# Odd chunks' inverse products on the other column half, six VectorE steps behind read-outs, and a shorter last unit in a FoX/RWKV-7 hybrid block

## The chip, the cores and the metric

The kernel runs on one core of a Trainium2 chip. Its engines work side by side, each through its own queue in order: TensorE (PE, with its weight loads as PEld), VectorE (DVE), ScalarE (ACT), GpSimd (POOL), and SyncE (SP), which mostly issues DMA transfers. The metric is the device time of one execution in microseconds; lower is better. The kernel before ran three times: 1635.21 (the median), 1632.43 and 1638.53 us.

## The reference

A transformer block for one sequence of 1024 tokens and width 1024: a token mixer with two branches (attention with a forget gate, and RWKV-7), gates, an output projection, and a feed-forward network with a short convolution. The change lies in the RWKV-7 branch, which has 8 heads of 64:

```python
def rwkv7_time_mix(p, mu, w0, w2, a0, a2, g2, k_k, k_a, r_k, ln_w, ln_b):
    p = p + (token_shift(p) - p) * mu
    r, k, v, xw, xa, xg = _split(p, RWKV_SPLITS)
    ...
    kk = heads(k * k_k)
    kk = kk / jnp.maximum(jnp.sqrt(jnp.sum(kk * kk, axis=-1, keepdims=True)), L2_EPS)
    k_mod = k.astype(jnp.float32) * (1 + (a - 1) * k_a)
    ...
    def step(state, inp):
        r_t, w_t, k_t, v_t, a_t, b_t = inp
        sa = jnp.einsum('bhvk,bhk->bhv', state, a_t)
        state = state * w_t[:, :, None, :] + sa[..., None] * b_t[:, :, None, :] + v_t[..., None] * k_t[:, :, None, :]
        y_t = jnp.einsum('bhvk,bhk->bhv', state, r_t)
        return state, y_t
    ...
    _, y = lax.scan(step, state0, ...)
    mean = jnp.mean(y, axis=-1, keepdims=True)
    var = jnp.mean(jnp.square(y - mean), axis=-1, keepdims=True)
    y = ((y - mean) * lax.rsqrt(var + GN_EPS)).reshape(bsz, seq, RWKV_WIDTH) * ln_w + ln_b
    bonus = (jnp.sum(r_h * k_h * r_k, axis=-1, keepdims=True) * v_h).reshape(bsz, seq, RWKV_WIDTH)
    return ((y + bonus) * g).astype(p.dtype)
```

## The kernel before

**Stages.** The span of 1632.7 us has a start with the modulation and the first projections (to about 160 us), the RWKV-7 chunk stage (about 160 to 622), attention (to about 815), and then the merge, the output projection and the feed-forward network. The change touches the chunk stage, and with the head loads at its end the start of attention.

**Units.** The recurrence isn't run step by step. The sequence is cut into chunks of 64 tokens, and within a chunk the recurrence becomes matrix products with the inverse of a unit triangular 64x64 matrix. The work goes in 8 units, numbered k = 0 to 7: four pairs p of heads, and for each the two halves hf of the sequence (8 chunks, `NCU`). The two heads of a pair lie on partitions 0 to 63 and 64 to 127 (`HS[0]`, `HS[1]`). The numbers in tile names give p and then the half or the chunk; the order's names end in a serial number.

**`pre`** (L745 to L875) prepares a unit. VectorE scales the keys and the decays (`kr`, `ar`, `al`, `bk`, and the bonus' `rkb`, which lies in the tile `ksq`). The products `p` of bk and ar give E, E's 32x32 diagonal blocks go by DMA through memory (`sm`, `M`), and 31 pairs of small VectorE steps (`t` at L828, `E` at L832) invert them in place. The inverse's blocks go back by DMA (`se`, `TT`). The transposes `vt`, `at`, `tb` and the product `q` fill UV and QA.

**`main`** (L877 to L985) finishes the inverse (`X`, `xi`, `zi`), multiplies it with QA (`uw`, L907 to L919), and copies one half of the result to Wt (VectorE) and the other to UV (ScalarE). Then come `mz` (which reads Wt), the chain of states (`sp`, `S`), the output `yp`, and the head-wise mean and variance (`mu`, `va`). `head_sums` splits a tile into a rounded part (`hi`, ScalarE; Ztr, Zts) and the rest (`lo`, L735; Wtr, Wts) and multiplies both by the block matrix `blk_r`.

**uw before.** For a chunk c and a head half h, rows `HS[h]` go to columns `HS[h]`: chunks 0 to 3 to one PSUM bank, 4 to 7 to the other. The trace lists each of these fp32 products as two records.

**What sets the order.** TensorE's order is the program's own: `Weave` interleaves the steps of `pre` and `main` with filler (the projections `ps_rkv`, `qk`, `v`, `gt`), and a generator's `yield x` lets some x ns of modelled filler pass first. The order of the other engines in this stage is set by a scheduler within the dependences; `tc.add_manual_dep(..., NOSYNC)` adds a dependence of order alone, with no wait on a semaphore between engines. `marks` holds the last instruction of a kind ("S", "E", "bank", "QA", "y") to which X is ordered. `evac_done` is called on each read-out of a filler's PSUM bank (`k`, `r`, `v` at L410, `vs` at L1002): the steps in `soft` that were emitted within the last 3000 modelled ns are ordered behind it.

The head loads `stA`, `stB` and `vh` of attention are issued from GpSimd's queue (L1043 to L1047), which also runs `lo` and the copies `hi_in` at L303.

Of the kernel before, what the change touches and what calls it, by code (L numbers as in the profile page):

```python
# [12 lines left out]
ALU = mybir.AluOpType  # L13
# [3 lines left out]
S = 1024  # L17
# [5 lines left out]
CH = 64  # L23
# [111 lines left out]
def hybrid_block(ctx: ExitStack, tc: tile.TileContext, a, out):  # L135
# [4 lines left out]
    def mm(o, lhsT, rhs, start, stop, more=False):  # L140

        weave.mm_cost(o, lhsT, rhs)
        nc.tensor.matmul(o, lhsT, rhs, start=start, stop=stop, skip_group_check=more)  # L143
# [5 lines left out]
    def f32(ap):  # L149
        return ap.bitcast(F32)  # L150
# [17 lines left out]
    def V(name, i=0, n=1):  # L168
        o, _ = VEC[name]
        return vec[:, o + i : o + i + n]  # L170
# [83 lines left out]
    def evac_done(i):  # L254
        for x, t in soft:
            if weave.now - t < 3000:
                tc.add_manual_dep(x.ins, i.ins.name, NOSYNC)
        soft.clear()
        return i
# [127 lines left out]
    with ExitStack() as es:  # L387
# [7 lines left out]
        def gen(name):  # L395
            return pr.tile([128, NH], F32, tag="gen", name=name)
# [318 lines left out]
        def c3(ap):  # L715
            return ap.rearrange("p (c s) -> p c s", s=CH)
# [13 lines left out]
        def head_sums(ps, x, hi, lo, behind_it=False):  # L730

            i = nc.scalar.copy(hi, x)
            if behind_it:
                behind_state(i)
            nc.gpsimd.tensor_tensor(lo, x, f32(hi), op=ALU.subtract)  # L735
            yield 3400
            mm(ps, blk_r, hi, start=True, stop=False)
            mm(ps, blk_r, lo, start=False, stop=True)

        def pre(k, p, hf):  # L740
# [40 lines left out]
            stt(kr, kr, V("k_k", p), al, op0=ALU.mult, op1=ALU.mult)  # L781
            tt(bk[:, :, 0, :], c3(kr), c3(en), op=ALU.mult)
            nc.gpsimd.tensor_copy(bk[64:128, :, 2, :], bk[64:128, :, 0, :])
            tt(ar[:, 1], c3(rr), el[:, :, 1:], op=ALU.mult)
            soft.clear()
            soft.append((ts(al, al, V("k_a", p), oka[:, p : p + 1], op0=ALU.mult, op1=ALU.add), weave.now))
            soft.append((tt(al, al, kk, op=ALU.mult), weave.now))
            soft.append((tt(bk[:, :, 1, :], c3(al), c3(en), op=ALU.mult), weave.now))
# [3 lines left out]
            stt(rkb, rr, V("r_k", p), al, op0=ALU.mult, op1=ALU.mult)  # L792
# [84 lines left out]
        def main(k, p, hf):  # L877
# [10 lines left out]
            for h in range(2):  # L888
                i = nc.vector.transpose(X[B0[h], :, :], TT[B0[h], :, 0:32])
                for x in ("S", "E", "bank") if k == 0 else ("S", "E", "QA") if k > 4 else ("S", "E"):  # L890
                    if x in marks:
                        tc.add_manual_dep(i.ins, marks[x].ins.name, NOSYNC)
# [17 lines left out]
            for c0 in range(0, NCU, 4):  # L910
                ps = gen(f"uw{n}{c0}")
                for c in range(c0, c0 + 4):
                    for h in range(2):
                        x = (c - c0) * 128
                        mm(ps[HS[h], x : x + 128], TT[HS[h], c, :], QA[HS[h], c, :, :], start=True, stop=True)
                pv = ps.rearrange("p (c a s) -> p c a s", a=2, s=CH)
                nc.vector.tensor_copy(Wt[:, c0 : c0 + 4, :], pv[:, :, 1, :])
                for h in range(2):
                    nc.scalar.copy(UV[HS[h], c0 : c0 + 4, h, :], pv[HS[h], :, 0, :])  # L919
# [44 lines left out]
            def part(nm, i):  # L964
                return rw.tile([128, NH], F32R, tag=nm, name=f"{nm}{i}{n}", bufs=1)
# [3 lines left out]
            yield from head_sums(mu, y, part("Zt", "r"), part("Wt", "r"))  # L969
            stt(y, mu, -1.0 / CH, y, op0=ALU.mult, op1=ALU.add)  # L970
            ysq = rw.tile([128, NH], F32, tag="ysq", name=f"ysq{n}", bufs=1)
            nc.scalar.activation(ysq, y, AF.Square)
            yield 2700
            va = gen(f"va{n}")
            yield from head_sums(va, ysq, part("Zt", "s"), part("Wt", "s"))
# [1150 lines left out]
```

## Time and profile before

| | |
|---|---|
| three runs, us | 1635.21, 1632.43, 1638.53 |
| the profiled execution, us | 1634.44 |
| its span in the trace, us | 1632.7 |
| mean granted TensorE clock | 0.996 |
| busy: TensorE, VectorE, ScalarE, GpSimd, us | 1598.9, 1211.9, 827.9, 155.5 |
| uw: products by the trace, us of one | 256 records, 0.269 |
| Wt copies: count, us of one | 16, 0.418 |

The profile is one execution. A row of the timeline gives the start, the duration of the group, engine, line, operation, out <- in, form and count; in brackets follows how long the engine was idle before it and what released it. In the form "64*64" is the part of TensorE's array that a product uses, rows by columns. A row of the groups gives the durations in ns (minimum, median, maximum). The chain of waits goes back from the last instruction to whatever released each step, so what stands in it set the time there; what doesn't had room.

### The profile page before, as it was taken

The page shows a single profiled execution, that of the slowest core. Times are in us where ns is not written, and L with a number is a line of the kernel's source. Part 1 is how long each engine was busy: PE and PEld are TensorE (multiplying, and loading weights), DVE is VectorE, ACT ScalarE, POOL GpSimd, SP SyncE. Part 2 cuts the span into 40 slices and gives each one's busy share as a digit, 9 for nine tenths or more (in the row PEclk, how much of TensorE's full clock was granted, in tenths as well). Part 3 has the DMA queues.
Part 4 walks back from the last instruction along what each step waited for, and adds up shares of the span by engine and source line. Part 5 has one row for each costly group of instructions (what it writes and reads, how often), then busy time and mean ns, then how long its engine had stood idle before and what let it go on. Part 6 is the DMA issues. An engine that isn't in the chain of part 4 may idle for free.

```text
span 1632.7 us, 25956 instructions
## 1 busy us (share of the span) xinstructions
PE 1598.9 (98%) x9678; PEld 1334.0 (82%) x9678; DVE 1211.9 (74%) x2343; ACT 827.9 (51%) x1557; POOL 155.5 (10%) x189
## 2 busy tenths in 40 slices
PE   7899999999999999999999999999999999999998
PEld 7777878888978788888888888888888888888886
DVE  4786787878876526878669548987777777886677
ACT  5563344544455656778623235644444444555455
POOL 0011111112111011333122000000000000000000
PEclk9999999999999999999999999999999999999999
DMA  9397645543333336434197511233322322675363
GB/s 341 120 337 206 178 132 148 136 117 93 112 106 95 98 126 161 130 108 123 49 345 277 189 70 39 78 129 102 118 97 97 110 98 97 237 246 162 123 213 110
DMA packets 123543, 238.79 MB, mean 146 GB/s; under 512 B 42189, under 2 KB 51285, under 8 KB 123417
## 3 DMA queue, kind: packets, MB, share of 16 engines
q1 hardware_dynamic: 114936, 218.77, 41.1%
q0 software_dynamic: 8480, 18.37, 4.2%
q8 instruction: 76, 1.25, 0.3%
q14 instruction: 51, 0.41, 0.1%
HBM read 172.57 MB, written 64.50 MB: 145 GB/s over the span
## 4 chain that ended last, share of the span: by engine, by line
PE 70%; DVE 7%; DMA 2%; ACT 2%; issue 2%; SPq 1%; POOL 0%; DVEq 0%; POOLq 0%; ACTq 0%
PE X L143 15%; PE D L143 13%; PE Y L143 7%; PE wo L143 5%; PE br L143 5%; PE gt L143 5%; PE W L143 4%; PE ps_rkv L143 3%; PE rk_ps L143 3%; PE ov L143 2%; PE lg L143 2%; PE tp L147 1%; DMA stB<-d_st 1%; DVE E L832 1%; DVE t L828 1%
## 5 line engine op out<-in xcount | busy, mean ns | idle before, releaser
L143 PE MATMUL D<-op,op 128*128 128x512 f32 x924 | 209.8, 389 | 0.0
L143 PEld LDWEIGHTS D<-op,op 128*128 128x128 f32 x924 | 173.3, 188 | 36.3 <-DVE op L1327 0.3
L143 PE MATMUL X<-T_m,S 128*128 128x512 f32 x440 | 107.1, 390 | 0.0
L143 PEld LDWEIGHTS X<-T_m,S 128*128 128x128 f32 x440 | 82.5, 188 | 17.7 <-ACT T_m L1809 0.5
L1326 ACT CAST op<-g 128x512 fp32r<-128x512 f32 x77 | 47.8, 621 | 72.9 <-PE D L143 47.6
L1327 DVE TENSOR_TENSOR op<-g,op 128x512 fp32r<-128x512 f32 x77 | 53.0, 689 | 41.2 <-ACT op L1326 41.2
L1588 DVE SCALAR_TENSOR_TENSOR c<-ab,vec,c 128x512 f32<-128x512 f32 x88 | 65.8, 750 | 18.4 <-ACT c L1591 16.8
L828 DVE TENSOR_TENSOR t<-E,M 128x60 f32<-128x60 f32 (+24 forms) x248 | 55.5, 224 | 24.3 <-DMA M<-sm 17.6
L1554 DVE TENSOR_TENSOR A<-ur,A 128x512 fp32r<-128x512 f32 x64 | 44.0, 689 | 38.3 <-ACT A L1550 38.2
L1554 DVE TENSOR_TENSOR S<-ur,S 128x512 fp32r<-128x512 f32 x66 | 45.5, 691 | 35.2 <-ACT S L1550 35.1
L1550 ACT CAST S<-ur 128x512 fp32r<-128x512 f32 x66 | 41.1, 622 | 57.3 <-DVE ur L1543 30.4
L311 DVE TENSOR_TENSOR lo_in<-raw_in,hi_in 128x512 fp32r<-128x512 f32 x84 | 57.6, 725 | 16.0 <-PE gt L143 4.8
L143 PE MATMUL Y<-T_h,A 128*128 128x512 f32 x264 | 63.4, 389 | 0.0
L143 PE MATMUL Y<-T_h,S 128*128 128x512 f32 x264 | 63.3, 389 | 0.0
L1140 DVE TENSOR_TENSOR tl<-tp,th 128x512 fp32r<-128x512 f32 (+1 forms) x80 | 50.0, 631 | 15.3 <-ACT th L1137 14.9
L1550 ACT CAST A<-ur 128x512 fp32r<-128x512 f32 x64 | 39.6, 621 | 42.9 <-PE X L143 31.3
L832 DVE TENSOR_TENSOR E<-E,t 128x60 f32<-128x60 f32 (+24 forms) x248 | 56.6, 228 | 6.3
L309 ACT CAST hi_in<-raw_in 128x1024 fp32r<-128x1024 f32 x42 | 43.8, 1048 | 33.3 <-PE qk L143 13.9
L143 PE MATMUL W<-B_f,A 128*128 128x512 f32 x252 | 60.6, 389 | 0.0
L143 PE MATMUL X<-B_b,A 128*128 128x512 f32 x252 | 60.5, 389 | 0.0
L143 PEld LDWEIGHTS Y<-T_h,S 128*128 128x128 f32 x264 | 49.6, 188 | 10.3
L143 PEld LDWEIGHTS Y<-T_h,A 128*128 128x128 f32 x264 | 49.6, 188 | 10.3
(499 smaller groups left out, 4137.7 us busy)
## 6 DMA issues: line engine op xcount, KB each, us to landing
raw_in<-in_w_in SPq DMA_DIRECT2D x50, 512.0 KB
wm<-in_w_mod SPq DMA_DIRECT2D x48, 512.0 KB
ur<-in_w_up SPq DMA_DIRECT2D x44, 512.0 KB
g<-d_g SPq DMA_DIRECT2D x35, 512.0 KB
d_g<-gs SPq DMA_DIRECT2D x44, 256.0 KB
d_g<-c SPq DMA_DIRECT2D x33, 256.0 KB
d_st<-qh SPq DMA_DIRECT2D x64, 128.0 KB
stA<-d_st POOLq DMA_DIRECT2D x8, 1024.0 KB, 8.2
```

Source lines behind the costliest of these rows:

```text
L143: nc.tensor.matmul(o, lhsT, rhs, start=start, stop=stop, skip_group_check=more)
L147: nc.tensor.transpose(o, i, eye)
L309: nc.scalar.copy(hi, raw)
L311: nc.vector.tensor_tensor(lo[:, c : c + NH], raw[:, c : c + NH], f32(hi[:, c : c + NH]), op=ALU.subtract)
L828: i = tt(tv, E32[:, 0:J, s : s + 1].to_broadcast([128, J, W]), M32[:, s : s + 1, s + 1 : 32].to_broadcast([128, J, W]), op=ALU.mult)
L832: tt(E32[:, 0:J, s + 1 : 32], E32[:, 0:J, s + 1 : 32], tv, op=ALU.add)
L1140: tt(tl[:, 0:w], tp[:, 0:w], f32(th[:, 0:w]), op=ALU.subtract)
L1326: nc.scalar.copy(hi, src)
L1327: tt(lo, src, f32(hi), op=ALU.subtract)
L1550: nc.scalar.copy(hi, src)
L1554: tt(lo, src, f32(hi), op=ALU.subtract)
L1588: stt(c, ab[:, x + hf * NH : x + hf * NH + NH], V("conv_w", 22 * x + i), c, op0=ALU.mult, op1=ALU.add)
```

## The change

It has four parts.

1. uw: the products of an odd chunk go from rows `HS[h]` to columns `HS[1 - h]`, into a bank of their own; even chunks stay. The two banks are now filled alternately, chunk by chunk. The even chunks' half of the result is copied to Wt in one VectorE copy of 128 partitions; of the odd chunks each head is copied across with a copy of its own (64 partitions), three copies instead of two. ScalarE's four copies to UV remain four.
2. `soft` is now cleared once in a unit and not at each read-out, and it holds six steps instead of three: kr, bk (from kr), al twice, bk (from al) and rkb.
3. In the last unit (k = 7) `lo` of both head sums is computed on VectorE instead of GpSimd, and the modelled filler ahead of mu and va is cut (3400 to 2300 for both, 2700 to 1200 for va).
4. In the sixth unit (k = 5) X is also ordered behind "y", which is now the last y that `main` subtracted the mean from.

```diff
@@ evac_done
         for x, t in soft:
             if weave.now - t < 3000:
                 tc.add_manual_dep(x.ins, i.ins.name, NOSYNC)
-        soft.clear()
         return i
@@ head_sums
-        def head_sums(ps, x, hi, lo, behind_it=False):
+        def head_sums(ps, x, hi, lo, behind_it=False, last=False):
...
-            nc.gpsimd.tensor_tensor(lo, x, f32(hi), op=ALU.subtract)
-            yield 3400
+            (nc.vector if last else nc.gpsimd).tensor_tensor(lo, x, f32(hi), op=ALU.subtract)
+            yield 2300 if last else 3400
@@ pre
-            stt(kr, kr, V("k_k", p), al, op0=ALU.mult, op1=ALU.mult)
-            tt(bk[:, :, 0, :], c3(kr), c3(en), op=ALU.mult)
+            soft.clear()
+
+            def easy(i):
+                soft.append((i, weave.now))
+
+            easy(stt(kr, kr, V("k_k", p), al, op0=ALU.mult, op1=ALU.mult))
+            easy(tt(bk[:, :, 0, :], c3(kr), c3(en), op=ALU.mult))
             nc.gpsimd.tensor_copy(bk[64:128, :, 2, :], bk[64:128, :, 0, :])
             tt(ar[:, 1], c3(rr), el[:, :, 1:], op=ALU.mult)
-            soft.clear()
-            soft.append((ts(al, al, V("k_a", p), oka[:, p : p + 1], op0=ALU.mult, op1=ALU.add), weave.now))
-            soft.append((tt(al, al, kk, op=ALU.mult), weave.now))
-            soft.append((tt(bk[:, :, 1, :], c3(al), c3(en), op=ALU.mult), weave.now))
+            easy(ts(al, al, V("k_a", p), oka[:, p : p + 1], op0=ALU.mult, op1=ALU.add))
+            easy(tt(al, al, kk, op=ALU.mult))
+            easy(tt(bk[:, :, 1, :], c3(al), c3(en), op=ALU.mult))
...
-            stt(rkb, rr, V("r_k", p), al, op0=ALU.mult, op1=ALU.mult)
+            easy(stt(rkb, rr, V("r_k", p), al, op0=ALU.mult, op1=ALU.mult))
@@ main
-                for x in ("S", "E", "bank") if k == 0 else ("S", "E", "QA") if k > 4 else ("S", "E"):
+                for x in ("S", "E", "bank") if k == 0 else ("S", "E", "QA", "y") if k == 5 else ("S", "E", "QA") if k > 5 else ("S", "E"):
...
-            for c0 in range(0, NCU, 4):
-                ps = gen(f"uw{n}{c0}")
-                for c in range(c0, c0 + 4):
-                    for h in range(2):
-                        x = (c - c0) * 128
-                        mm(ps[HS[h], x : x + 128], TT[HS[h], c, :], QA[HS[h], c, :, :], start=True, stop=True)
-                pv = ps.rearrange("p (c a s) -> p c a s", a=2, s=CH)
-                nc.vector.tensor_copy(Wt[:, c0 : c0 + 4, :], pv[:, :, 1, :])
+            ps = [gen(f"uw{n}{e}") for e in range(2)]
+            for c in range(NCU):
                 for h in range(2):
-                    nc.scalar.copy(UV[HS[h], c0 : c0 + 4, h, :], pv[HS[h], :, 0, :])
+                    x = c // 2 * 128
+                    mm(ps[c % 2][HS[h ^ c % 2], x : x + 128], TT[HS[h], c, :], QA[HS[h], c, :, :], start=True, stop=True)
+            pv = [x.rearrange("p (c a s) -> p c a s", a=2, s=CH) for x in ps]
+            nc.vector.tensor_copy(Wt[:, 0::2, :], pv[0][:, :, 1, :])
+            for h in range(2):
+                nc.vector.tensor_copy(Wt[HS[h], 1::2, :], pv[1][HS[1 - h], :, 1, :])
+            for e in range(2):
+                for h in range(2):
+                    nc.scalar.copy(UV[HS[h], e::2, h, :], pv[e][HS[h ^ e], :, 0, :])
...
-            yield from head_sums(mu, y, part("Zt", "r"), part("Wt", "r"))
-            stt(y, mu, -1.0 / CH, y, op0=ALU.mult, op1=ALU.add)
+            yield from head_sums(mu, y, part("Zt", "r"), part("Wt", "r"), last=k == 7)
+            marks["y"] = stt(y, mu, -1.0 / CH, y, op0=ALU.mult, op1=ALU.add)
...
-            yield 2700
+            yield 1200 if k == 7 else 2700
             va = gen(f"va{n}")
-            yield from head_sums(va, ysq, part("Zt", "s"), part("Wt", "s"))
+            yield from head_sums(va, ysq, part("Zt", "s"), part("Wt", "s"), last=k == 7)
```

**How the order moves: VectorE at unit 0's Wt copies.** The steps t and E are those of unit 1's inverse. Before, and then with the change:

```order
L828 TENSOR_TENSOR t_1_1927<-E_1_1925,M_1_1920 128x75
L917 COPY Wt_0_2277<-uw_00_2278 128x256
L832 TENSOR_TENSOR E_1_1925<-E_1_1925,t_1_1927 128x5x15
L828 TENSOR_TENSOR t_1_1927<-E_1_1925,M_1_1920 128x70
L832 TENSOR_TENSOR E_1_1925<-E_1_1925,t_1_1927 128x5x14
L917 COPY Wt_0_2277<-uw_04_2290 128x256
L828 TENSOR_TENSOR t_1_1927<-E_1_1925,M_1_1920 128x65
```

```order
L831 TENSOR_TENSOR t_1_1927<-E_1_1925,M_1_1920 128x75
L835 TENSOR_TENSOR E_1_1925<-E_1_1925,t_1_1927 128x5x15
L831 TENSOR_TENSOR t_1_1927<-E_1_1925,M_1_1920 128x70
L835 TENSOR_TENSOR E_1_1925<-E_1_1925,t_1_1927 128x5x14
L919 COPY Wt_0_2277<-uw_00_2278 128x4x64
L831 TENSOR_TENSOR t_1_1927<-E_1_1925,M_1_1920 128x65
L921 COPY Wt_0_2277<-uw_01_2279 64x4x64 x2
```

The first copy moves behind three steps of the inverse, and one more step (t, 128x65) now stands ahead of the last two copies. In units 2, 6 and 7 the three copies stand together. TensorE's order around uw changes only in that the two banks alternate: `uw_00 x2`, `uw_01 x2`, four times, in place of `uw_00 x8`, `uw_04 x8`.

**VectorE at the start of unit 5** (X of unit 5's inverse, y of unit 4). Before, and then with the change:

```order
L857 COPY QA_0_5099<-at_0_5270 64x4x64 x4
L889 STREAM_TRANSPOSE X_1_5383<-TT_1_4630 32x256
L970 SCALAR_TENSOR_TENSOR y_0_5152<-mu_0_5154,y_0_5152 128x512
L889 STREAM_TRANSPOSE X_1_5383<-TT_1_4630 32x256
L869 COPY QA_0_5099<-q_0_5320 128x8x64
L828 TENSOR_TENSOR t_0_5194<-E_0_5192,M_0_5187 128x31
```

```order
L860 COPY QA_0_5104<-at_0_5275 64x4x64 x4
L975 SCALAR_TENSOR_TENSOR y_0_5157<-mu_0_5159,y_0_5157 128x512
L892 STREAM_TRANSPOSE X_1_5388<-TT_1_4634 32x256 x2
L872 COPY QA_0_5104<-q_0_5325 128x8x64
L831 TENSOR_TENSOR t_0_5199<-E_0_5197,M_0_5192 128x31
```

Only y has moved, ahead of both X; t, and behind it gs, stay where they were.

**TensorE in the last unit** (gt is the filler; mu and va are unit 7's). Before, and then with the change:

```order
L143 MATMUL gt_1_6738<-u_hi,lo_in_6532 128x512 x3
L143 MATMUL mu_1_6729<-Ztr_1_6742,blk_r 128x512
L143 MATMUL mu_1_6729<-Wtr_1_6743,blk_r 128x512
L143 MATMUL gt_1_6738<-u_hi,lo_in_6532 128x512 x5
L143 MATMUL gt_0_6786<-u_hi,hi_in_6673 128x512 x8
L143 MATMUL gt_0_6786<-u_lo,hi_in_6673 128x512 x8
L143 MATMUL gt_0_6786<-u_hi,lo_in_6674 128x512 x8
L143 MATMUL va_1_6795<-Zts_1_6796,blk_r 128x512
L143 MATMUL va_1_6795<-Wts_1_6797,blk_r 128x512
```

```order
L143 MATMUL gt_1_6746<-u_lo,hi_in_6539 128x512 x6
L143 MATMUL mu_1_6737<-Ztr_1_6750,blk_r 128x512
L143 MATMUL mu_1_6737<-Wtr_1_6751,blk_r 128x512
L143 MATMUL gt_1_6746<-u_lo,hi_in_6539 128x512 x2
L143 MATMUL gt_1_6746<-u_hi,lo_in_6540 128x512 x8
L143 MATMUL gt_0_6799<-u_hi,hi_in_6681 128x512 x7
L143 MATMUL va_1_6776<-Zts_1_6777,blk_r 128x512
L143 MATMUL va_1_6776<-Wts_1_6778,blk_r 128x512
```

mu stands 5 filler matmuls sooner, and between mu and va there are 17 in place of 29. From attention on, TensorE's order is the same in both kernels.

## The prediction

> **What bounds the kernel now.** I read the page's engine table first, then the busy time by stage, then what TensorE waited for in the stage that the change touches, then the chain of waits there. The first two show what there is to win (of a stretch: its length, then the busy time of PE, of its weight loads, DVE, ACT and POOL).
>
> ```profile
> span 1632.7 us, 25956 instructions
> PE 1598.9 (98%) x9678; PEld 1334.0 (82%) x9678; DVE 1211.9 (74%) x2343; ACT 827.9 (51%) x1557; POOL 155.5 (10%) x189
> ...
> 160.00:340.70 180.70, 178.76 (x1633) 148.17 (x1631) 148.96 (x423) 78.10 (x146) 25.21 (x39) 1.00 0.52 141
> ...
> 404.00:468.00 64.00, 60.71 (x692) 53.69 (x690) 49.28 (x144) 29.22 (x63) 9.13 (x12) 1.00 0.39 114
> 468.00:593.00 125.00, 124.34 (x1141) 102.09 (x1143) 77.43 (x203) 70.63 (x133) 10.35 (x11) 1.00 0.29 92
> ```
>
> The matmuls of the chunk stage (160 to 622 us) leave TensorE idle for little: 1.9 us up to 340.7, 3.3 from 404 to 468, 0.7 from there to 593. So waits alone can give some 6 us; anything more must come from matmuls that take less time. TensorE's waits in that stage, from the table of who waited for whom (total, times, longest):
>
> ```profile
> PE v L143 <- DVE vs L1002: 1.6, 2, 1.1
> PE va L143 <- POOL Wts L735: 0.9, 1, 0.9
> ...
> PE zi L143 <- ACT X L899: 0.6, 1, 0.6
> PE ps_rkv L143 <- DVE k L410: 0.6, 1, 0.6
> PE va L143 <- ACT Zts L732: 0.6, 1, 0.6
> PE lg L143 <- DMA stB<-d_st: 0.3, 1, 0.3
> ```
>
> A busy TensorE is not a binding one, since a matmul that is done early may only wait longer at the next place. The chain of waits tells where it binds. Pieces of it (start, length, what):
>
> ```profile
> 339.29 0.74 DVE ksq L792
> 340.19 0.44 DVE vs L1002
> 340.67 0.98 PE v L143 x6
> ...
> 372.57 1.89 PE uw L143 x32
> ...
> 424.28 0.34 DVE Wt L917
> ...
> 459.84 2.60 DMA M<-sm
> ...
> 463.88 0.61 DVE gs L380
> ...
> 467.60 0.37 ACT X L899
> ...
> 471.22 1.90 PE uw L143 x32
> ...
> 603.14 18.33 DMA stB<-d_st
> ```
>
> Four stretches follow. Up to 340.67 VectorE sets the pace (units 0 to 2 of eight). From there to 404 it is TensorE (unit 3). From 404 to 468 VectorE sets it, and then the transfers around the inverse (unit 4 and the start of 5). From 471 on it is TensorE (units 5 to 7), until the last unit's end, where the chain hangs on the landing of stB. I price the change in each stretch by what sets its pace.
>
> **The odd chunks' products (uw).** Before, all chunks' products of head half h go from rows h to columns h, so two tiles of the array run at a time and the other two stand idle; now each even chunk has an odd one beside it on the idle two.
>
> ```profile
> L143 PE MATMUL uw<-QA,TT x256: 269/269/320, 228.7 to 569.7; 64*64 64x128 f32 x128
> 228.71 1.96 PE L143 MATMUL uw<-QA,TT 64*64 64x128 f32 x32
> ...
> 454.40 1.15 PE L143 MATMUL q<-UV,E 64*64 64x64 f32 x32
> ...
> L143 PE MATMUL mpb<-acc,cst x16: 379/391/403, 123.9 to 139.5; 128*32 128x256 f32 x16
> 123.90 0.64 PE L143 MATMUL mpb<-acc,cst 128*32 128x256 f32 x8
> ```
>
> A unit's 32 records (16 products, each listed twice) take 1.96 us; less the last one's 0.269, 15 steps of a pair are 1.69, or 0.113 a step. If four run at once, there are 8 steps for 16: 8 x 0.113 = 0.90 us less a unit, 7.2 in eight. That is the upper bound; the lower is nothing. No row of this kernel shows four 64*64 tiles at once. The nearest is mpb: eight records of 0.39 each in 0.64, so four on the same rows and different columns went together. And q, with half the columns, starts a pair every (1.15 - 0.27) / 15 = 0.06 us, so weights can be loaded at twice the rate that uw uses now. I take the full 0.90.
>
> [...]
>
> **What of it counts.** The 0.90 goes on to the end only if TensorE doesn't wait at the next product that needs VectorE: mz, which reads Wt. The change makes Wt later. It takes three copies for two, since the odd chunks' halves cross and need one copy each, and on VectorE's queue all of them now stand where the second copy stood, with one step (t) among them.
>
> ```profile
> 233.49 0.42 DVE L917 COPY Wt<-uw 128x256 f32<-128x256 f32 x1
> 233.82 0.22 DVE L828 TENSOR_TENSOR t<-E,M 128x65 f32<-128x65 f32 x1
> 234.04 0.55 PE L143 MATMUL mz<-E,Wt 64*64 64x128 f32 x6
> ...
> 376.69 0.42 DVE L917 COPY Wt<-uw 128x256 f32<-128x256 f32 x1
> 377.83 1.96 PE L143 MATMUL mz<-E,Wt 64*64 64x128 f32 x32
> ...
> 474.80 0.42 DVE L917 COPY Wt<-uw 128x256 f32<-128x256 f32 x1
> 476.46 1.96 PE L143 MATMUL mz<-E,Wt 64*64 64x128 f32 x32
> ...
> 452.43 0.87 DVE L857 COPY QA<-at 64x256 f32<-64x256 f32 x2
> ```
>
> Two copies of 64 partitions take 0.87, or 0.43 each, and one of 128 takes 0.42: half the partitions save nothing. So Wt ends 0.42 (the third copy) + 0.22 (t) = 0.64 later, and mz is wanted 0.90 earlier. The room from the last Wt copy's end to mz before was 234.04 - 233.91 = 0.13 in unit 0, 0.72 in unit 3, 1.24 in unit 5. TensorE then waits 0.64 + 0.90 less that room: 1.41, 0.82, 0.30. Of the 0.90, unit 0 keeps -0.5, unit 3 +0.1 and unit 5 +0.6. Units 6 and 7 I give the full 0.90 each, since their order has no t among the copies and VectorE is lightly loaded there (77.43 us of 125). In the order of the stretches: units 0 to 2 lie where VectorE sets the pace, so uw's gain there counts for nothing and the added copy costs 0.42 for each unit whose copies lie ahead of 340.67 on the chain, at most 3 x 0.42 = +1.3. Unit 3 gives -0.1. Unit 4's copies are on the chain: +0.4. Units 5 to 7 give -0.6 - 0.9 - 0.9 = -2.4.
>
> **Six steps behind the read-outs.** These are the same instructions in another order; nothing is added. The waits of ps_rkv on k (0.6) and the first of v on vs (0.5 of the 1.6) stand behind such steps: in the chain above ksq runs just ahead of vs. In the new order k passes two of them and vs all six, at some 0.7 each as ksq's row has it, though steps of the inverse (t and E, some 0.2 each) take part of their places; either is more than the wait. So 1.1 us of TensorE's idle time go, within the stretch where VectorE paces. Since the six still have to run before the next unit's products p, the gain lies between 1.1 and nothing. With the added copies the first stretch lies between +1.3 and -1.1, and I take -0.6: the chain leaves VectorE at a read-out, and that is what gets earlier. The second wait of v (1.1) I leave as it is.
>
> **The transposition X behind y (unit 5).** VectorE before ran X, y, X, and X had to wait for its transfer.
>
> ```profile
> 451.83 0.39 PE L143 MATMUL mu<-Wtr,blk_r 128*128 128x512 f32 x1
> ...
> 456.49 0.43 DVE L889 STREAM_TRANSPOSE X<-TT 32x256 f32<-32x256 f32 x1 [3.20 <-DMA TT<-se]
> 456.95 0.69 DVE L970 SCALAR_TENSOR_TENSOR y<-mu,y 128x512 f32<-128x512 f32 x1
> ```
>
> The input of y, mu, is complete by 452.2, so y can run when the copies of QA end, at 453.3, in place of 456.95, and both waits of va (0.6 + 0.9, in the table above) go. But this moves the wait. The next bank that TensorE needs is read by gs, which on VectorE stands behind t, and t waits for M (459.84 + 2.60 in the chain); zi stands behind gs, rs and the copies of X, the last of which ends at 467.97. None of these starts sooner because of y. So the 1.5 us are waited out at ps_rkv and zi: net 0, bounded by -1.5. The stretch from 404 to 468 gets the added copy alone: +0.4, less what the easy steps give back in it. I take +0.2.
>
> **The last unit.**
>
> ```profile
> 601.17 1.30 POOL L735 TENSOR_TENSOR Wts<-ysq,Zts 128x512 fp32r<-128x512 f32 x1 [4.62 <-ACT Zts L732]
> 602.41 0.73 POOL L1043 DMA_DIRECT2D stA<-d_st  x1
> ...
> 621.52 0.50 PE L143 MATMUL lg<-stB 68*128 68x512 f32 x1 [0.34 <-DMA stB<-d_st]
> ```
>
> The subtraction goes from GpSimd (1.30) to VectorE, whose y of the same shape takes 0.69, and va stands 17 matmuls sooner. But va is not waited for here, and what fills TensorE is the same work in another order. The head loads no longer stand behind Wts on GpSimd's queue and are issued at least 1.3 earlier. That ends the wait of 0.34 for stB: -0.3. Later stages keep their order, and I leave them alone.
>
> **Sum.** -0.6 - 0.1 + 0.2 - 2.4 - 0.3 = -3.2 us. The profiled execution took 1634.4 (span 1632.7 and 1.7 around it), so 1631.2 by its own scale. The median of the three runs, 1635.2, lies 0.8 higher: 1632.0.
>
> **Rivals.**
>
> Everything lands. If VectorE has more room than its chain says, uw's 7.2, the waits of k and v (0.6 + 1.6), of va (1.5) and of stB (0.3) all go: -11.2, or 1624. For it: TensorE is 98% busy and even a VectorE-paced piece hides only 1.9 us of idle in 180.7. Against: the rooms of 0.13 and 0.72 at mz. Chance 0.14.
>
> Four tiles don't run at once. If the odd pair's weights can't be loaded while the even pair streams through the same rows, uw stays at 1.96 us, units 3 and 5 to 7 give nothing, and the copies stay: -0.6 + 0 + 0.2 + 0 - 0.3 = -0.7, or 1634.5. For it: no row shows all four quarters at once. Against it: mpb. Chance 0.16. [...] That the waits only move, as argued for va, would give about the same.
>
> VectorE becomes the bound, slower. The place is Wt ahead of mz in each unit; the price is the added copy, 8 x 0.42 = 3.4, and the step t ahead of mz, 8 x 0.22 = 1.8, since mz feeds Zt, Mt and the states' chain behind it: +5.2, or 1640. It decides the time where Wt's end passes the old start of mz, which by the rooms holds in unit 0 (0.13 < 0.64) and not in unit 3 (0.72). VectorE's 148.96 us of 180.70 speak for it, its 77.43 of 125 against. Chance 0.12.
>
> The forecast, with part of the gain kept, has the remaining 0.58.
>
> **How the numbers follow.** About 0.5% (8.2 us) is what a measurement of this kernel tells from no change. Under my forecast the time lies in 1627 to 1636. With the first rival's lower side at 1624 and the last one's 1640 less its tail, the range is 1624.5 to 1639. Faster by over 8.2 us comes from the first rival (0.14) and a tail of the forecast (0.03). Slower by over 8.2 would need more than the last rival's 5.2, so I give half of its chance, 0.06, and 0.02 for what I don't see. The rest, 0.75, is no change that could be told.
>
> **What would show it.** In the changed profile: a unit's uw x32 in about 1.06 us and not 1.96 (else the second rival); three Wt copies of about 0.42; a new wait of mz on Wt, over 1 us in unit 0 and none in units 6 and 7; no wait of ps_rkv on k near 245 nor of va near 460, and in place of the latter a longer wait at ps_rkv or zi near 465 to 468; no wait for stB at 621. The forecast is wrong if the stage from 160 to 622 gets longer, or shorter by over 8 us.

## The result, and the profile after

The change made the kernel slower, and by more than the range allowed: the median is 1642.86 us (six runs, 1641.47 to 1644.49) against 1633.80 for the kernel before (six runs, 1632.38 to 1638.53). The ratio is 1.0052, with a 95% interval of 1.0037 to 1.0066, or 6 to 11 us. The forecast was 1632.0, the range 1624.5 to 1639.

The head of the page after the change, its span and busy times:

```profile
span 1639.7 us, 25964 instructions
PE 1595.5 (97%) x9678; PEld 1327.1 (81%) x9678; DVE 1216.2 (74%) x2353; ACT 828.0 (50%) x1557; POOL 156.5 (10%) x187
```

The span grew by 7.0 us (from 1632.7), though TensorE is busy 3.4 us less: uw's matmuls do take less time (1.10 us a unit, 1.96 before). So TensorE waits more, and the table of who waited for whom, from 160 us to 640 (total, times, longest), names waits that weren't there before, among them:

```profile
PE rk_ps L143 <- DVE gs L379: 5.0, 1, 5.0
PE ps_rkv L143 <- DVE gs L379: 2.3, 1, 2.3
PE va L143 <- POOL Wts L734: 1.5, 1, 1.5
...
PE mz L143 <- DVE t L831: 0.6, 1, 0.6
PE v L143 <- DVE vs L1007: 0.6, 1, 0.6
...
PE mz L143 <- DVE Wt L919: 0.5, 1, 0.5
```

The first, at rk_ps, stands in the last unit and is the subject of this section; the others are of the kinds that the prediction speaks of, and come back below. The chain of waits leads from it to a transfer (start, length, what):

```profile
602.03 13.38 DMA gg<-d_lora
...
615.50 0.69 DVE gg L988
616.19 0.61 DVE gs L379
...
616.84 7.58 PE rk_ps L143 x24
```

gg is a load of 256 KB: the values with which the last y is multiplied. Four queues side by side in the timeline after the change (start, duration, engine, line, what; in brackets the idle time before and its releaser):

```profile
591.78 0.73 POOL L1048 DMA_DIRECT2D stA<-d_st  x1 [39.10 <-ACT S L955]
...
594.08 0.71 POOL L1048 DMA_DIRECT2D stA<-d_st  x1
...
602.03 0.32 SPq L982 DMA_DIRECT2D gg<-d_lora  x1
...
604.77 0.75 DVE L987 SCALAR_TENSOR_TENSOR y<-y,vec,bon 128x512 f32<-128x512 f32 x1
615.50 0.69 DVE L988 TENSOR_TENSOR gg<-y,gg 128x512 f32<-128x512 f32 x1 [9.97 <-DMA gg<-d_lora]
616.10 0.68 DVE L379 SCALAR_TENSOR_TENSOR gs<-gt,gs 128x512 f32<-128x512 f32 x1
...
616.84 3.78 PE L143 MATMUL rk_ps<-u_hi,hi_in 128*128 128x512 f32 x8 [4.95 <-DVE gs L379]
620.42 2.19 PE L143 MATMUL rk_ps<-u_lo,hi_in 128*128 128x512 f32 x8
622.44 1.98 PE L143 MATMUL rk_ps<-u_hi,lo_in 128*128 128x512 f32 x8
```

And the same places before, in that kernel's timeline:

```profile
602.49 0.32 SPq L977 DMA_DIRECT2D gg<-d_lora  x1
...
608.81 0.69 DVE L983 TENSOR_TENSOR gg<-y,gg 128x512 f32<-128x512 f32 x1
...
610.45 0.70 POOL L1043 DMA_DIRECT2D stA<-d_st  x1
```

Read downwards: the head loads, once held up on GpSimd's queue by Wts (head 0) and by a copy hi_in (head 1), now go out back to back from 591.78 on. gg is issued 0.46 us sooner than before, so at nearly the same time. Before, of the head loads only the first (head 0's stA) was issued ahead of it, by 0.08 us; now both heads' are, by 6 us and more, and gg lands 13.4 us after its issue. VectorE stands at gg for 9.97 us (it also gets there 3.2 us sooner than before, since va does), and in its queue behind gg stands gs, the read-out that frees the PSUM bank for rk_ps. TensorE waits 4.95 us there, and then runs eight matmuls in 3.78 us and eight in 2.19 that otherwise take 1.98 each. The busy time by stretch shows why (length, then PE, PEld, DVE, ACT, POOL, and after them the granted clock, the DMA share and GB/s):

```profile
605.00:610.00 5.00, 5.00 (x24) 4.14 (x23) 0.53 (x1) 1.86 (x3) 0.00 (x0) 1.00 1.13 311
610.00:615.00 5.00, 1.89 (x9) 1.23 (x7) 0.00 (x0) 0.00 (x0) 1.04 (x1) 0.89 0.61 158
615.00:620.00 5.00, 3.16 (x8) 2.51 (x9) 1.99 (x3) 2.38 (x4) 0.00 (x0) 0.50 0.49 164
```

After the wait the clock was granted at 0.50. So the place costs 4.95 + 1.80 + 0.21 = 7.0 us, as much as the span grew. (Spans of single executions also differ by their start: the chunk stage's first product begins at 162.0 us in the profile before and at 159.5 in the one after. The lead is gone by the last unit's mz, which starts at 573.31 before and 573.48 after, so the 7.0 arise behind it. Where a few us matter, the ratios decide.)

### The profile page after: what moved, and what is told of

Read it like the earlier page. It is cut to its first block, busy times and chain, and to the rows that moved or that the text cites. A ratio compares the mean times of both kernels' runs of the same rounds, so it can differ in the third digit from the quotient of the medians.

```text
span 1639.7 us, 25964 instructions
## 1 busy us (share of the span) xinstructions
PE 1595.5 (97%) x9678; PEld 1327.1 (81%) x9678; DVE 1216.2 (74%) x2353; ACT 828.0 (50%) x1557; POOL 156.5 (10%) x187
## 4 chain that ended last, share of the span: by engine, by line
PE 70%; DVE 7%; DMA 2%; ACT 2%; issue 1%; SPq 1%; POOL 0%; DVEq 0%; POOLq 0%; ACTq 0%
PE X L143 15%; PE D L143 13%; PE Y L143 7%; PE wo L143 5%; PE br L143 5%; PE gt L143 4%; PE W L143 4%; PE rk_ps L143 3%; PE ps_rkv L143 3%; PE ov L143 2%; PE lg L143 2%; PE tp L147 1%; PE v L143 1%; DVE t L831 1%; DMA gg<-d_lora 1%
## 5 line engine op out<-in xcount | busy, mean ns | idle before, releaser
L308 ACT CAST hi_in<-raw_in 128x1024 fp32r<-128x1024 f32 x42 | 43.8, 1048 | 32.9 <-PE qk L143 13.4
```

Source lines behind the costliest of these rows:

```text
L308: nc.scalar.copy(hi, raw)
```

## The experiments

Each run is compared with runs of the kernel before on the same chip. "The change" is the kernel above.

### Which part costs the time

**e1_without_last**: the change without its third part.

```diff
-            yield from head_sums(mu, y, part("Zt", "r"), part("Wt", "r"), last=k == 7)
+            yield from head_sums(mu, y, part("Zt", "r"), part("Wt", "r"))
...
-            yield 1200 if k == 7 else 2700
+            yield 2700
...
-            yield from head_sums(va, ysq, part("Zt", "s"), part("Wt", "s"), last=k == 7)
+            yield from head_sums(va, ysq, part("Zt", "s"), part("Wt", "s"))
```

> The change without its third part (the last unit keeps GpSimd's subtractions and the longer filler). Theory A, the load of gg waits behind the head loads that are now issued 8 us sooner, and TensorE with it: the loss goes, ratio to before 0.998 to 1.002, VectorE's wait for gg (10.0 us) and the wait of rk_ps (5.0 us) are gone and the granted clock from 593 to 622 us is 1.00 again. Theory B, the third Wt copy and the later place of all of them on VectorE make each unit longer: the ratio stays at 1.004 to 1.006.

Measured: 1635.73, ratio 1.0008 (0.9998 to 1.0017); no wait at gg or rk_ps.

**e2_last_alone**: the kernel before with the third part alone (the lines above the other way round).

> The kernel before with the third part alone. Theory A: slower as the whole change is, ratio 1.003 to 1.006, with a wait of some 10 us of VectorE for gg and of some 5 us at rk_ps. Theory B: no slower than before, ratio 0.998 to 1.001, since uw and its copies are untouched.

Measured: 1641.79, ratio 1.0045 (1.0028 to 1.0061); VectorE waits 10.1 us for gg and TensorE 5.1 for gs. The third part makes the loss, alone or with the others. What is left, 1.0008, is no gain either where -2.9 us (0.998) had been predicted.

**e4_uw_alone**, **e8_soft_alone**, **e9_xy_alone**: the kernel before with one of the other parts each, as in the diff of the change.

> The kernel before with the first part alone (odd chunks' uw on the other column half, three Wt copies). Theory A, with the forecast's sum: uw 1.10 us and not 1.96, part of it kept, ratio 0.997 to 1.000. Theory B: ratio above 1.002, with waits of mz on Wt in most units.

> The kernel before with the second part alone, six steps behind the read-outs. The forecast's step: the waits of ps_rkv on k (0.6) and of v on vs at 340 us (0.5) go, ratio 0.9993 to 1.0. The rival: what the read-outs gain the next unit's products p lose, so that waits of p, q or E take their place and the ratio is 1.0 or above.

> The kernel before with the fourth part alone, X of unit 5 behind y. The forecast's step: both waits of va near 460 us (1.4) go, and a wait of 1 to 2 us at ps_rkv for VectorE's gs, which stands behind t and the landing of M, takes their place, with zi as late as before (467.6); ratio 0.9995 to 1.0005. The rival: the 1.4 us are won for good, ratio 0.9985 to 0.9995 and no wait at ps_rkv.

Measured: uw alone 1636.81, ratio 1.0010 (1.0000 to 1.0019); the six steps 1636.54, 1.0000 (0.9989 to 1.0010); X behind y 1636.55, 1.0003 (0.9994 to 1.0012). None gains by itself.

### How the last unit loses it

**e3_gg_early**: the change, with unit 7's gg in a tile of its own and loaded ahead of yp.

```diff
+            if k == 7:
+                gg = rw.tile([128, NH], F32, tag="cum", name=f"gg{n}", bufs=1)
+                nc.sync.dma_start(gg, d_lora[2, p, :, cs])
             yp = py.tile([128, NCU, CH], F32, tag="yp", name=f"yp{n}")
...
-            gg = rw.tile([128, NH], F32, tag="ysq", name=f"gg{n}", bufs=1)
-            nc.sync.dma_start(gg, d_lora[2, p, :, cs])
+            if k < 7:
+                gg = rw.tile([128, NH], F32, tag="ysq", name=f"gg{n}", bufs=1)
+                nc.sync.dma_start(gg, d_lora[2, p, :, cs])
```

> The whole change, with the last unit's load of gg put into the tile of cum, which is free by then, and issued ahead of that unit's yp, long before the head loads; everything else stays, the head loads 8 us sooner among it. Theory A: gg is there in time, the wait at rk_ps goes, ratio 0.997 to 1.001. Theory B: ratio 1.004 to 1.006 as for the whole change. A third way, C: the head loads slow TensorE in some other manner (the weights of gt and rk_ps, raw_in, come late): the wait moves to another tile and the ratio stays above 1.003.

Measured: 1635.11, ratio 1.0000 (0.9991 to 1.0009); the waits at gg and rk_ps are gone, though the head loads go out as early as in the change. So neither their own issue nor VectorE's extra work costs anything that can be told: it is gg's place behind them. (raw_in, 512 KB, stands ahead of gg on SyncE's queue in all these kernels. It isn't the cause alone: in e5, next, it is issued 0.55 us ahead of gg as in the change, and TensorE doesn't wait.)

**e5_head1_behind_gg**: the change, with head 1's loads held back until gg is used.

```diff
-            tt(gg, y, gg, op=ALU.mult)
+            marks["gg"] = tt(gg, y, gg, op=ALU.mult)
...
-        nc.gpsimd.dma_start(A, d_st[h, 0:2, :, :].rearrange("k r s -> r k s"))
+        i = nc.gpsimd.dma_start(A, d_st[h, 0:2, :, :].rearrange("k r s -> r k s"))
+        if h == 1:
+            tc.add_manual_dep(i.ins, marks["gg"].ins.name, mybir.DependencyInfo(mybir.DependencyClass.Sync, mybir.DependencyReason.DATA))
```

> The whole change, but the second head's loads (stA, stB, vh) wait for VectorE's product gg of the last unit; the first head's stay 8 us sooner, and gg is loaded as late as in the change. Theory A1, what delays gg is the bulk that is in flight when it is issued at 602 us: with one head's 2.1 MB in place of 4.2 ahead of it, gg lands before 607 and VectorE waits for it under 2 us; ratio 0.998 to 1.002. Theory A2, it is enough that any head load lies ahead on the transfer engines: the wait stays near 10 us and the ratio above 1.003.

Measured: 1635.95, ratio 0.9998 (0.9989 to 1.0007). Its timeline on VectorE and GpSimd:

```profile
611.94 0.69 DVE L988 TENSOR_TENSOR gg<-y,gg 128x512 f32<-128x512 f32 x1 [4.31 <-DMA gg<-d_lora]
...
612.93 0.70 POOL L1048 DMA_DIRECT2D stA<-d_st  x1 [16.74 <-DVE gg L988]
```

With half of the bulk ahead of it, gg is waited for 4.31 us in place of 9.97. That is more than I expected of head 0's loads alone, yet gs now ends before rk_ps needs its bank, and TensorE doesn't wait for it at all: the 4.31 us fitted in that room.

**e10_last_yields**: the kernel before with the third part's shorter filler alone; GpSimd keeps lo.

```diff
-            yield 3400
+            yield 2300 if last else 3400
...
-            yield 2700
+            yield 1200 if k == 7 else 2700
```

> The kernel before with the third part's shorter filler alone; GpSimd keeps the subtractions, so the head loads stay behind Wts on its queue, though Wts comes some 3 us sooner. If it is the move to VectorE that frees the head loads, gg is issued with them and not 10 us behind them, VectorE waits for it under 1 us and the ratio is 0.999 to 1.001. If the shorter filler does the harm (va too early for its inputs, or both heads' loads in flight), there is a wait of over 1 us at va or rk_ps and the ratio is above 1.002.

Measured: 1639.30, ratio 1.0018 (1.0009 to 1.0028), between the two ratios that I had named, with the wait of the second. The head loads stay behind Wts on GpSimd's queue, but the shorter filler brings head 1's to directly behind head 0's: its timeline has head 1's stA at

```profile
604.51 0.72 POOL L1043 DMA_DIRECT2D stA<-d_st  x1
```

instead of 610.45, in one burst around gg's issue at 603.35. VectorE's and TensorE's waits in it:

```profile
DVE gg L983 <- DMA gg<-d_lora: 7.3, 1, 7.3
...
PE rk_ps L143 <- DVE gs L380: 2.3, 1, 2.3
```

So with e5 it is the second head's 2 MB in the time of gg's transfer that make TensorE wait, whether they are issued before gg or right after. The subtraction's move isn't needed for a loss; with it the loss is larger (1.0045 in e2).

**b4_last_mended**: the kernel before with the third part and gg early.

> The kernel before with the third part and with the last unit's gg loaded early into the tile of cum. If the third part's only harm is gg's late landing, no wait for gg nor for stB is left and the ratio is 0.999 to 1.0005, against 1.0045 for the third part alone. If the burst of both heads' loads harms otherwise, a wait of over 1 us stays after 600 us and the ratio is above 1.001.

Measured: 1635.38, ratio 0.9996 (0.9987 to 1.0006), no wait for gg nor for stB. So mending the last unit brings it back to the kernel before, and the 0.3 us that I had counted for stB are too few to be told.

### Where the other gains went

First two places in the trace of the change itself. TensorE at the start of unit 5, where the prediction had the waits of va moving to ps_rkv and zi:

```profile
464.28 3.43 PE L143 MATMUL ps_rkv<-u_hi,hi_in 128*128 128x512 f32 x8 [2.31 <-DVE gs L379]
467.64 0.81 PE L143 MATMUL zi<-TT,X 32*32 32x32 f32 x32
```

The waits of va (1.5) have become one of 2.31 at ps_rkv, and zi doesn't wait; but the eight matmuls behind the wait take 3.43 us in place of 1.98, and zi starts at 467.64, where before it started at 467.63. And in the middle of unit 5, on GpSimd and TensorE:

```profile
504.42 3.18 POOL L787 COPY bk<-bk 64x512 f32<-64x512 f32 x1 [5.79 <-DVE bk L786]
507.68 1.60 POOL L734 TENSOR_TENSOR Wts<-ysq,Zts 128x512 fp32r<-128x512 f32 x1
...
509.34 0.51 PE L143 MATMUL va<-Wts,blk_r 128*128 128x512 f32 x1 [1.51 <-POOL Wts L734]
```

The copy of bk takes 3.18 here, while VectorE runs one operation with two inputs after another, and Wts behind it on GpSimd's queue is late for va. Before, the copy took 0.77, and VectorE stood idle for 0.28 us beside it:

```profile
504.09 0.77 POOL L783 COPY bk<-bk 64x512 f32<-64x512 f32 x1 [4.79 <-DVE bk L782]
...
504.68 0.73 DVE L311 TENSOR_TENSOR lo_in<-raw_in,hi_in 128x512 fp32r<-128x512 f32 x1 [0.28 <-ACT ysq L972]
```

The runs that follow all load gg early, so that the last unit is out of the way.

**e6_mz_by_parity**: mz's banks hold even and odd chunks as uw's do, so that its first half needs the first Wt copy only.

```diff
-            for c0 in range(0, NCU, 4):
-                ps = gen(f"mz{n}{c0}")
-                for c in range(c0, c0 + 4):
+            for e in range(2):
+                ps = gen(f"mz{n}{e}")
+                for c in range(e, NCU, 2):
```

> As the kernel with gg early, and mz also goes by parity: the even chunks' products first, which need the first Wt copy alone, then the odd ones. If the waits of mz on the later copies are what eats uw's gain, those in units 0, 1 and 3 (0.5 to 1.2 us each with the slowed products) go and the ratio falls by 0.001 to 0.002 against the kernel with gg early (1.000). If VectorE and the transfers set the pace there, the waits move to v, q and ps_rkv and the ratio stays within 0.0007 of it.

Measured: 1634.97, ratio 0.9991 (0.9981 to 1.0000). mz no longer waits for the odd chunks' copies, and bk's copy takes 0.77 in this run; but ps_rkv waits 3.0 us for gs. That wait was 2.6 in e3, so a part of what is won at mz is waited out at a later read-out; the step from e3 (0.0009) lies within the intervals.

**e7_bk_on_scalar**: gg early, and the copy of bk on ScalarE instead of GpSimd.

```diff
-            nc.gpsimd.tensor_copy(bk[64:128, :, 2, :], bk[64:128, :, 0, :])
+            nc.scalar.copy(bk[64:128, :, 2, :], bk[64:128, :, 0, :])
```

> As the kernel with gg early, and the copy of half of bk goes from GpSimd to ScalarE. If the wait of va for Wts in unit 6 (0.95 us there, 1.5 in the change) comes from that copy, which takes 3.18 us near 504 us in every kernel with the new uw and 0.77 in the kernel before, Wts starts some 2 us sooner, the wait goes, and the ratio falls by some 0.0005, which the interval can't tell: it is read from the trace. If Wts itself is slow, the wait stays.

Measured: 1639.71, ratio 1.0021 (1.0011 to 1.0032): slower. va's wait goes, but the copies of the states S queue behind bk's on ScalarE, and TensorE waits for them in five places:

```profile
PE sp L143 <- ACT S L958: 5.5, 5, 1.6
```

**b3_odd_copies_on_scalar**: e6 with the odd chunks' Wt copies on ScalarE, so that VectorE has one copy less than before.

```diff
-                nc.vector.tensor_copy(Wt[HS[h], 1::2, :], pv[1][HS[1 - h], :, 1, :])
+                nc.scalar.copy(Wt[HS[h], 1::2, :], pv[1][HS[1 - h], :, 1, :])
```

> As the kernel with mz by parity and gg early, but the two crossing Wt copies of the odd chunks run on ScalarE, so VectorE has one Wt copy a unit, one fewer than the kernel before. If VectorE's added copies are what gives uw's gain back, the waits of mz near 233 and 281 us shrink below 0.3 us, the ratio to before falls to 0.998 or below (some 3 us). If VectorE's chain and the transfers set the pace whatever uw does, the ratio stays between 0.9985 and 1.0005 and the wait of ps_rkv near 464 us grows by what is won ahead of it.

Measured: 1634.96, ratio 0.9997 (0.9987 to 1.0007); ps_rkv waits 3.2 us for gs. Taking the added copies off VectorE gains nothing. That doesn't clear them wholly, since on ScalarE they meet the copies of the states: sp waits 1.4 us for S in this run, where it waits 0.8 in e6.

**b1_gs_ahead** and **b2_gs_ahead_old_uw**: gs is ordered ahead of the step t that waits for M at the start of unit 5; b1 is e6 with it, b2 the change with gg early, with it, and with uw and mz as they were before.

```diff
-            stt(g, ps, 0.0, g, op0=ALU.min, op1=ALU.subtract)
+            read = stt(g, ps, 0.0, g, op0=ALU.min, op1=ALU.subtract)
+            for x in waiting:
+                tc.add_manual_dep(x.ins, read.ins.name, NOSYNC)
+            waiting.clear()
...
+                if k == 6 and s == 0:
+                    waiting.append(i)
```

> As the kernel with mz by parity and gg early, and VectorE's first gs goes ahead of the inverse's first step t in unit 5, which waits for M. If the wait of ps_rkv near 464 us (3.0) is what absorbs the gains of units 0 to 4, it falls under 1 us, X and zi come some 2 us sooner, and the ratio to before is 0.997 to 0.9985. If the transfers of M set the pace there anyway, the wait moves to the next products of that unit and the ratio stays at 0.999.

> As the kernel with gs ahead, but with uw and mz as in the kernel before: the second, third and fourth part, gg early and gs ahead remain. If uw's 6.9 us count for something once that wait is gone, this one is slower than the one with gs ahead by 0.001 or more. If the same steps of VectorE and GpSimd set the pace of both, the two ratios differ by less than 0.0007.

Measured: 1637.29, ratio 1.0010 (1.0001 to 1.0019), and 1636.68, ratio 1.0002 (0.9992 to 1.0012). The wait at ps_rkv is gone in both, yet nothing is gained: in both va now waits longer for Wts. Nor is the kernel with the old uw the slower one, as it would be if uw's shorter time counted here; it is 0.0008 lower, with intervals that overlap. The table of waits of b2 has

```profile
PE va L143 <- POOL Wts L738: 2.5, 1, 2.5
```

and GpSimd's copy of bk in it takes 3.18 us again. So the long copy doesn't belong to the new uw, as I had thought at e7: b2 has the old one, while e6 has the new one and 0.77.

**b5_vector_wts** and **b6_vector_wts_new_uw**: b2 and b1 with Wts of unit 5 on VectorE, past GpSimd's queue.

```diff
-            (nc.vector if last else nc.gpsimd).tensor_tensor(lo, x, f32(hi), op=ALU.subtract)
+            (nc.vector if last or vec else nc.gpsimd).tensor_tensor(lo, x, f32(hi), op=ALU.subtract)
...
-            yield from head_sums(va, ysq, part("Zt", "s"), part("Wt", "s"), last=k == 7)
+            yield from head_sums(va, ysq, part("Zt", "s"), part("Wt", "s"), last=k == 7, vec=k == 5)
```

> The kernel with gs ahead of t and the old uw, with the rest Wts of unit 5's variance computed on VectorE in place of GpSimd. Theory (the gain of a sooner gs is eaten behind GpSimd's stretched copy of bk, where va waits 2.5 us for Wts): va's wait falls below 0.5 us and the ratio to the kernel before is about 0.998. Rival (VectorE sets the pace of units 4 to 6, and a wait taken away at one place comes back at the next): another wait of 1.5 us or more stands between 464 and 530 us, and the ratio is 1.000 within 0.001.

> The same edit on the kernel with gs ahead of t and the new uw. Theory: va's wait falls below 0.5 us, the ratio to the kernel before is 0.997 to 0.999, below that of the run with the old uw. Rival: the wait comes back at mz or the next read-out, and the ratio is 1.000 within 0.001, no better with the new uw than with the old.

Measured: 1632.87, ratio 0.9984 (0.9975 to 0.9993), and 1635.06, ratio 0.9992 (0.9983 to 1.0001). In b5's table of waits, va is down to two short ones:

```profile
PE mz L143 <- DVE Wt L926: 1.2, 1, 1.2
...
PE va L143 <- DVE Wts L738: 0.5, 2, 0.3
```

and from 462 to 470 TensorE doesn't idle, at a granted clock of 1.00:

```profile
462.00:470.00 8.00, 8.00 (x87) 6.28 (x86) 5.80 (x20) 4.26 (x9) 0.00 (x0) 1.00 0.40 110
```

Taking Wts off GpSimd's queue moved the ratio by -0.0018 with the old uw (b2 to b5) and by -0.0018 with the new (b1 to b6), some 3 us each, with intervals that just touch. So the gain from a sooner gs was eaten at that one place, as far as two steps of this size can show it. The forecast for b6 fell, though: with the new uw it is no better than with the old (0.9992 against 0.9984), and a wait of 1.8 us stands at mz. b5, with the change's first part left out, is the one version here that is faster than the kernel before by more than its interval; against the change itself the two ratios make it 0.68%, or 11 us.

## Why the prediction was wrong

**The step that failed: the last unit.** I priced it as: "The head loads no longer stand behind Wts on GpSimd's queue and are issued at least 1.3 earlier. That ends the wait of 0.34 for stB: -0.3." The first half happened, by more than I said (10.6 us for head 0, 16.4 for head 1), and the wait for stB went. What I left out is which transfer the loads get ahead of. I looked at the consumer of the loads and never at the other load that is due in the same microseconds, gg, issued from another queue at a nearly unchanged time. Its price was 7.0 us in the profile in place of -0.3, and e1, e2, e3 and e5 show by taking away the part, the rest, gg's place and the second head's loads in turn that this is the cause; e10 brings the second head's loads in without moving the subtraction, and the same wait comes. I also said "Later stages keep their order, and I leave them alone"; that was right for the order of the program, but the order of the transfers is not in it.

**uw at four tiles: right.** 32 records take 1.10 us where I said 1.06, and 1.96 before. (The rival in which four tiles don't run at once would have left 1.96.) First uw and then mz of unit 0, and the copies of odd chunks as a group:

```profile
228.44 1.10 PE L143 MATMUL uw<-QA,TT 64*64 64x128 f32 x32
...
233.44 0.43 PE L143 MATMUL mz<-E,Wt 64*64 64x128 f32 x4 [0.47 <-DVE Wt L919]
234.03 2.19 PE L143 MATMUL mz<-E,Wt 64*64 64x128 f32 x28 [0.16 <-DVE Wt L921]
...
L921 DVE COPY Wt<-uw x16: 418/422/427, 233.6 to 571.1; 64x256 f32<-64x256 f32 x16
```

**Waits of mz: right.** In unit 0 mz loses 0.47 ahead and ends 2.78 us after its start where it took 1.96, so 1.29 in all (said: 1.41); in unit 3 0.83 (0.82), in unit 5 0.29 (0.30), none in 6 and 7. Unit 1, which I had not worked out, loses 1.4 in the same way (0.65 ahead of mz, which then takes 2.70). The copies take 0.42 each, as said.

**Six steps behind the read-outs: the place right, the worth wrong.** The wait of ps_rkv on k is gone and those of v are down to 0.6, but e8, the part alone, has a ratio of 1.0000 with new waits at mu (1.3) and va (1.5). I had named nothing gained as one bound, and took -0.6 for the whole first stretch, added copies included.

**X behind y: right in direction, short in size.** The waits moved on to ps_rkv, as argued, net 0 (e9: 1.0003). I expected 1.5 us; it is 2.3, and the eight matmuls behind it run slower as well (3.43 us in place of 1.98), at a granted clock of 0.50 that I had not priced.

**Units 5 to 7: wrong.** I gave them -2.4, since TensorE sets the pace there and Wt has room in units 6 and 7. Against the kernel before, mz ends 0.83 us sooner in unit 5, 1.08 later in unit 6 and 0.17 later in unit 7. So unit 7 kept its 0.9, and the loss lies between unit 5's mz and unit 6's, in two places. The first is va in unit 5 (1.51, behind GpSimd's stretched copy); b5 and b6 show that this wait costs. The second I overlooked: I took mz for the next product behind uw that needs VectorE, but in unit 6 q stands ahead of mz, and q reads UV. First before, then with the change:

```profile
518.08 1.96 PE L143 MATMUL uw<-QA,TT 64*64 64x128 f32 x32
...
521.27 0.97 PE L143 MATMUL q<-UV,E 64*64 64x64 f32 x26
```

```profile
519.04 1.10 PE L143 MATMUL uw<-QA,TT 64*64 64x128 f32 x32
519.15 1.73 DVE L860 COPY QA<-at 64x256 f32<-64x256 f32 x4 [2.09 <-PE at L147]
520.91 0.42 DVE L919 COPY Wt<-uw 128x256 f32<-128x256 f32 x1
521.37 0.74 ACT L924 COPY UV<-uw 64x256 f32<-64x256 f32 x2 [0.83 <-DVE Wt L919]
522.16 1.15 PE L143 MATMUL q<-UV,E 64*64 64x64 f32 x32 [0.46 <-ACT UV L924]
```

While uw runs, VectorE copies QA for 1.73 us; the copies to Wt and UV follow, and q after them. None of these got shorter. From uw's start to q's it is 3.19 us before, 3.12 with the change and 3.12 in b6: of uw's 0.86, 0.07 is left. Why the new uw gains nothing even in b6 is so explained in part, by this and by the 1.8 us at mz there; the rest stays open. The forecast's sum without the last unit was -2.9; measured is 1.0008 (e1), or +1.3, within -0.3 and +2.8.

**The rivals.** None was the outcome. The one that ended slower put the price at Wt ahead of mz; b3, which takes the added copies off VectorE, measures no difference for it. What came was of the kind that I had left 0.02 for, a place that I didn't see.

## What to carry to other kernels

When a transfer is issued sooner, list what else is due from memory in the time that it fills, on every queue, and ask which engine stands still if that comes late, and what is queued behind it. Issue the small load that is needed first ahead of the bulk (here one line, e3, took back all of the loss: 1.0000 in place of 1.0052), or hold the bulk until the small one is used (e5, 0.9998). And price what follows a wait too: behind the one of 2.31 us here, which took the place of 0.6 and 0.9, the granted clock was 0.50, and zi started no sooner (467.64 us, 467.63 before). When a product gets shorter, follow every product behind it to the copies that it reads, not the first alone (here q in unit 6).

## What the runs showed of the hardware

**A small load beside bulk.** gg's 256 KB landed 13.38 us after their issue behind both heads' loads (the change). With both issued around it VectorE could use gg 9.7 us after its issue (e10), behind one head's, issued 8 to 10 us ahead, 7.8 (e5), and beside head 0's alone 6.3 us were enough (before). From 600 to 616 us the change's transfers by queue were (packets, MB, share of the 16 engines):

```profile
q0 software_dynamic: 990, 2.33, 65.1%
q1 hardware_dynamic: 568, 1.30, 31.0%
```

q0 is the bulk; q1 holds gg and SyncE's other transfers, among them a load of 512 KB (raw_in) issued 0.55 us ahead of gg. In the last five microseconds ahead of 615 the engines were busy only 0.61 of the time, so the sum of bytes doesn't explain gg's landing; what it waited for inside the queues stays open.

**The clock after a wait.** Behind 4.95 us of idle the granted clock was 0.50 (the change, 615 to 620 us), and behind 2.31 us too: eight matmuls took 3.43 us, and the stretch reads

```profile
464.00:467.00 3.00, 2.72 (x6) 2.15 (x7) 2.62 (x14) 2.72 (x5) 0.00 (x0) 0.50 0.40 119
```

In e9 the clock was 0.56 in the two microseconds behind 2.08 us of idle (3.59 for the eight). The length of the wait alone doesn't tell: mz's products behind a wait of 2.15 us in b1 ran at a granted clock of 1.00. What else decides is not shown here.

**GpSimd's copy beside VectorE.** The copy of 64x512 took 0.77 us before, where VectorE stood idle for 0.28 us beside it, and 0.77 in e6. It took 3.18 in the change and in b2, where VectorE ran operations with two inputs beside it without a gap, and 3.78 in b5. Why the copy takes longer there is not shown here.
